# Part of a convolution moved to ScalarE and accumulating transfers, and a projection block moved between attention heads

## The chip, the cores and the metric

The kernel runs on one core of a Trainium2 chip. The metric is device time in microseconds of one execution. Three runs of the kernel before took 1779.26, 1779.52 and 1779.70 us; the median, 1779.52, is the time before. The engines are called as the profile calls them: PE (TensorE, matrix products; PEld its weight loads), DVE (VectorE), ACT (ScalarE), POOL (GpSimd) and SP (the queue that issues most transfers). Each engine works through its own list of instructions in order and waits on semaphores for the others.

## The reference

Two layers over 512 tokens of width 1024. Each layer normalises its input, projects it with one wide matrix, and feeds three token mixers whose outputs are gated and merged; then follow a feed-forward part and a gated embedding. What this case is about lies in the mixers:

```python
for i in range(DEPTH):
    h = rmsnorm(x, norm_mix[i])
    qa, ka, va, glu_in, qc, kc, vc, gates = split(h @ w_in[i])
    ya = diff_attention(qa, ka, va, ...)          # 4 heads, softmax difference, rmsnorm per head
    yb = conformer_conv(glu_in, ...)
    yc = neighbourhood_attention(qc, kc, vc, rpb[i])
    ga, gb, gc = split(sigmoid(gates))
    merged = ga * (ya @ w_br_a[i]) + gb * (yb @ w_br_b[i]) + gc * (yc @ w_br_c[i])
    x = x + merged @ w_o[i]
    ...

def conformer_conv(u, conv_w, conv_b, cln_g, cln_b):
    a, g = split(u)
    z = a * sigmoid(g)                            # 512 channels
    z = conv(z, conv_w) + conv_b                  # 31 taps, each channel by itself
    return silu(layernorm(z, cln_g, cln_b))
```

## The kernel before, in words

Activations lie transposed: 128 channels on the partitions, 512 tokens along the free axis, so a projection makes one 128x512 block at a time. A product in fp32 is made of three products of shorter numbers: every operand is split into a high half (ACT copies it with rounding, line 147) and a low half (DVE subtracts, line 161), and PE multiplies high by high, high by low, low by high (lines 181 to 183). `weights` fetches a block of weights by SP into a raw tile `wr` and splits it into `wh` and `wl`; there are three tiles of each tag, so the next block's split can start when PE or DVE has finished with the tile three blocks earlier.

A layer runs in this order: the gated input of the convolution (`glu`), neighbourhood attention (`natten`), the differential attention's projections and heads (`diff`), the gate blocks of the third mixer (`gate_c`, 8 blocks), two gate blocks of the second (`gate_b`), the product of the third mixer (`branch_c`, 8 blocks), two more blocks of `gate_b`, the product of the first mixer with its gates (`merge_a`, 8 blocks), the end of the convolution (`conv`) among the last four blocks of `gate_b`, then the merge, `w_o`, the feed-forward part and the embedding.

The order of PE's instructions is written by hand: it is the order of the Python code. Attention heads are cut into units, generators that a queue starts after so many blocks of products (`later`, `tick`), so pieces of a head stand between projection blocks. The order of DVE, ACT, POOL and SP is set by a scheduler that goes by the position in the program and by declared priorities; weights carry a priority of 400 positions ahead.

The 124 taps of the convolution (4 groups of 128 channels, 31 taps each) are DVE instructions: the first of a group at line 549, the others at line 164, one fused multiply and add of 128x512 into the group's sum. `taps` is a generator, and `background(after, n)` takes the next n taps from it and places them behind a given instruction. The table `BG` says how many each phase places. When `conv` starts, it takes the taps that are left, adds the four groups (`conv_ss`), splits the sum into `conv_rp`, and PE multiplies it with a matrix of ones (lines 579 and 580) for the mean.

A norm (`norm`) is four transposes on PE (line 217), a sum on DVE (line 220), a small step on DVE, a power on POOL (line 227, tile `rc`) and four transposes that spread the result (line 231). Transposes go through PSUM tiles of the tag `tr`, of which there are two; DVE frees such a tile when it has written the low half of what is in it (`diff_pt`).

Small tiles have a fixed number of buffers by tag: seven of the tag `t` (among them `diff_t`, the unnormalised output of a head, and `mergea_t`), two of the tag `b`. In the feed-forward part POOL issues transfers that add weights from memory to a tile (line 995).

Of the kernel before, what the change touches and what calls it, by code (L numbers as in the profile page):

```python
# [14 lines left out]
AF = mybir.ActivationFunctionType  # L15
ALU = mybir.AluOpType
# [4 lines left out]
P = 128  # L21
# [3 lines left out]
GR = 8  # L25
D = 1024
KD = 8
# [3 lines left out]
CON3W = 31  # L31
# [14 lines left out]
PAR_L = 8 + 8 + 8 + 1 + 4 + 4 + 4 + 4 * CON3W  # L46
PAR = L * PAR_L + 8
WARM = 8
BG = dict(glu=2, natten=1, values=3, diff=1, gatec=2, branchc=2, gateb=4, mergea=4, mergea2=2)
FIRST = (["v"] * 4 + ["pt"] * 2 + ["y", "b"], ["y"] * 5 + ["pt"] * 2 + ["b"])  # L50
EARLY = 6
QUARTERS = (2, 4, 6)
# [13 lines left out]
class Net:  # L66
# [229 lines left out]
    def build(self):  # L296
        nc, tc, a = self.nc, self.tc, self.a
        self.bufs = dict(wr=3, wh=3, wl=3, h=8, qk=2, kh=2, v=4, pt=2, y=5, z=5, x=4, t=7, rp=4,
                         e=4, a=3, r=2, rb=1, ss=1, sm=8, rc=4, b=2, s=8)
        self.bg, self.w_ahead = BG, 400  # L300
        self.pbufs = dict(mm=3, sc=2, tr=2, av=1)
# [130 lines left out]
    def layer(self, i, h, xsrc, xs):  # L432
        self.i, self.h = i, h
        zs, cs = [], []
        self.todo = self.taps(zs, cs)
        self.glu(zs)
        if i == 0:
            self.lambdas()
        yc, ya, yb = [], [], []
        sn, sd = {}, {}  # L440
        self.natten_in(0, sn, yc)
        self.drain(self.renorm)
        self.h = self.hs
        self.natten_v(sn)
        last = self.glu_last(zs)
        self.natten_in(1, sn, yc)
        next(last)
        self.natten_in(2, sn, yc)
        next(last)
        self.natten_in(3, sn, yc)  # L450
        acc, gb = [], []
        self.diff_in(0, sd, ya)
        self.diff_v(0, sd)
        self.diff_in(1, sd, ya)
        self.gate_c(acc, 0)
        self.diff_v(1, sd)
        self.diff_in(2, sd, ya)
        self.diff_in(3, sd, ya)
        for m in range(1, KD):
            self.gate_c(acc, m)  # L460
        for m in range(2):
            self.gate_b(gb, m, AF.Copy, None)
        for g in acc + gb:
            self.act(g, g, AF.Sigmoid, table="sigmoid")
        self.branch_c(acc, yc)
        for m in range(2, 4):
            self.gate_b(gb, m, AF.Sigmoid, "sigmoid")
        self.merge_a(ya, acc)
        conv = self.run(self.conv(cs, yb))
        pairs = self.inputs()  # L470
        for m in range(4, KD):
            self.gate_b(gb, m, AF.Sigmoid, "sigmoid")
            for n in ((0, 1), (2,), (3,), ())[m - 4]:
                self.input_block(pairs, n)
        self.drain(conv)
        mg = self.merge_b(yb, acc, gb)
        ws = self.pair_weights(4)
        x, h = self.w_o(mg, xsrc)
        self.input_pair(ws, pairs, 4)
        h = self.ffn(h, x)  # L480
        return self.ple(h, x, xs, self.inputs())
# [57 lines left out]
    def taps(self, zs, cs):  # L539

        for j, z in enumerate(zs):
            zf = z.rearrange("p a b -> p (a b)")
            c = self.sb("z", [P, 512])
            cs.append(c)
            for d in range(CON3W):
                w = self.par(self.i, "cw", j * CON3W + d)
                src = zf[:, d * GR:d * GR + 512]
                if d == 0:
                    yield self.nc.vector.tensor_scalar(c, src, w, self.par(self.i, "cb", j),
                                                       ALU.mult, ALU.add)  # L550
                else:
                    yield self.stt(c, src, w, c, ALU.mult, ALU.add)

    def background(self, after, n):

        ph, self.phase = self.phase, "conv"
        for _ in range(n):
            i = next(self.todo, None)
            if i is not None:
                self.tc.add_manual_dep(  # L560
                    i.ins, after.ins.name,
                    mybir.DependencyInfo(mybir.DependencyClass.NoSync, mybir.DependencyReason.DATA),
                    reason="background")
        self.phase = ph
# [203 lines left out]
    def gate_c(self, acc, m):  # L768
        self.phase = "gatec"
        ps = self.proj(OFF_G + 2 * D + m * P)  # L770
        if m % 2 == 0:
            acc += self.parts_of("x", [512], 2)
        self.background(self.act(acc[m], ps, AF.Copy), self.bg["gatec"])

    def branch_c(self, acc, ys):
        self.phase = "branchc"
        for m in range(KD):
            ps = self.ps("mm")
            self.gemm(ps, self.a["w_br_c"][self.i, m], ys)
            self.background(self.tt(acc[m], acc[m], ps, ALU.mult), self.bg["branchc"])  # L780

    def merge_a(self, ys, acc):
        self.phase = "mergea"
        for m in range(KD):
            ps = self.proj(OFF_G + m * P)
            g = self.sb("t", [P, 512])
            self.background(self.act(g, ps, AF.Sigmoid, table="sigmoid"), self.bg["mergea"])
            pb = self.ps("mm")
            self.gemm(pb, self.a["w_br_a"][self.i, m], ys)
            self.tt(g, g, pb, ALU.mult)  # L790
            self.background(self.tt(acc[m], acc[m], g, ALU.add), self.bg["mergea2"])

    def gate_b(self, gs, m, func, table):
        self.phase = "gateb"
        ps = self.proj(OFF_G + D + m * P)
        if m == 0:
            gs += [self.sb("kh", [P, 512]) for _ in range(2)]
        elif m % 2 == 0:
            gs += self.parts_of("v", [512], 2)
        self.background(self.act(gs[m], ps, func, table=table), self.bg["gateb"])  # L800

    def merge_b(self, ys, acc, gs):
        self.phase = "mergeb"
        out = []
        for m in range(KD):
            pb = self.ps("mm")
            self.gemm(pb, self.a["w_br_b"][self.i, m], ys)
            self.tt(gs[m], gs[m], pb, ALU.mult)
            self.tt(acc[m], acc[m], gs[m], ALU.add)
            mg = self.sb("y" if m < 5 else "v", [P, 2, 512], F32R)  # L810
            self.split(mg[:, 0, :], mg[:, 1, :], acc[m])
            out.append(mg)
        return out
# [656 lines left out]
```

## Time and profile before

| | |
|---|---|
| median of three runs | 1779.52 us |
| the profiled execution | 1779.11 us |
| its span, first to last instruction | 1777.3 us |
| mean granted TensorE clock | 0.998 |
| PE, PEld, DVE, ACT, POOL busy | 99%, 87%, 80%, 50%, 5% |
| DVE's taps of line 164 | 240, 747 ns each, 179.3 us |

The profile's rows read: start in us, duration in us, engine, line, operation, output and inputs by the program's names, shape; in brackets the idle time before the instruction and what ended it. The row of a wait says who waited for whom, then microseconds in total, the number of times and the longest. Tile names carry the phase in front: `conv_ss` is the tile `ss` made in the phase `conv`. Matmuls overlap, so that a row's duration of 0.39 us goes with a spacing of 0.227 us.

### The profile page before, as it was taken

The page shows a single profiled execution, that of the slowest core. Times are in us where ns is not written, and L with a number is a line of the kernel's source. Part 1 is how long each engine was busy: PE and PEld are TensorE (multiplying, and loading weights), DVE is VectorE, ACT ScalarE, POOL GpSimd, SP SyncE. Part 2 cuts the span into 40 slices and gives each one's busy share as a digit, 9 for nine tenths or more (in the row PEclk, how much of TensorE's full clock was granted, in tenths as well). Part 3 has the DMA queues.
Part 4 walks back from the last instruction along what each step waited for, and adds up shares of the span by engine and source line. Part 5 has one row for each costly group of instructions (what it writes and reads, how often), then busy time and mean ns, then how long its engine had stood idle before and what let it go on. Part 6 is the DMA issues. An engine that isn't in the chain of part 4 may idle for free.

```text
span 1777.3 us, 26765 instructions
## 1 busy us (share of the span) xinstructions
PE 1760.8 (99%) x9954; PEld 1544.1 (87%) x9954; DVE 1413.5 (80%) x2354; ACT 893.4 (50%) x1529; POOL 97.4 (5%) x114
## 2 busy tenths in 40 slices
PE   9999999999999999999999999999999999999998
PEld 7888878888899899998888887888888998989987
DVE  7967887998898587787776688779887985877776
ACT  5576555325565254454545765452356643534444
POOL 0000000000111010100000000000001110101000
PEclk9999999999999999999999999999999999999999
DMA  6577541334757366544446765423256673655332
GB/s 224 162 186 186 170 132 43 110 99 139 227 156 190 113 166 158 137 124 128 154 134 174 183 177 156 115 67 99 94 172 202 176 178 111 178 135 159 99 104 95
DMA packets 113698, 258.12 MB, mean 145 GB/s; under 512 B 14496, under 2 KB 23456, under 8 KB 113568
## 3 DMA queue, kind: packets, MB, share of 16 engines
q1 hardware_dynamic: 100176, 232.03, 42.7%
q0 software_dynamic: 12672, 23.07, 8.2%
q8 instruction: 78, 1.28, 0.3%
q10 hardware_dynamic: 720, 1.31, 0.2%
q14 instruction: 52, 0.43, 0.1%
HBM read 218.60 MB, written 7.34 MB: 127 GB/s over the span
## 4 chain that ended last, share of the span: by engine, by line
PE 90%; DVE 5%; ACT 1%; DMA 1%; issue 1%; SPq 0%; POOL 0%; ACTq 0%; DVEq 0%; POOLq 0%
PE ffn_mm L1025 4%; PE ffn_mm L1027 4%; PE ffn_mm L181 4%; PE ffn_mm L183 4%; PE ffn_mm L182 4%; PE ffn_mm L1026 4%; PE ffn_sc L1027 3%; PE ffn_sc L1025 3%; PE ffn_sc L1026 3%; PE mergea_mm L181 2%; PE mergea_mm L183 2%; PE mergea_mm L182 2%; PE gateb_mm L181 2%; PE wo_mm L181 2%; PE wo_mm L183 2%; PE wo_mm L182 2%
## 5 line engine op out<-in xcount | busy, mean ns | idle before, releaser
L164 DVE SCALAR_TENSOR_TENSOR conv_z<-glu_z,pre_par,conv_z 128x512 f32<-128x512 f32 x240 | 179.3, 747 | 3.0
L147 ACT ACTIVATE ffn_wh<-ffn_wr 128x1024 fp32r<-128x1024 f32 (+1 forms) x92 | 92.7, 1014 | 111.3 <-PE ffn_mm L182 80.7
L161 DVE TENSOR_TENSOR ffn_wl<-ffn_wr,ffn_wh 128x1024 fp32r<-128x1024 f32 (+1 forms) x92 | 107.3, 1172 | 5.4 <-ACT ffn_wh L147 4.9
L995 POOL DMA_DIRECT2D ffn_qk<-w_fu x88 | 77.9, 980 | 603.3 <-DMA ffn_qk<-w_fu 299.6
L161 DVE TENSOR_TENSOR ffn_t<-ffn_mm,wo_rb 128x512 f32<-128x512 f32 (+1 forms) x64 | 38.6, 604 | 67.8 <-PE ffn_mm L183 67.8
L147 ACT ACTIVATE mergea_wh<-mergea_wr 128x1024 fp32r<-128x1024 f32 (+1 forms) x32 | 27.1, 848 | 91.2 <-PE mergea_mm L182 71.7
L147 ACT ACTIVATE ffn_wh<-ffn_qk 128x1024 fp32r<-128x1024 f32 x44 | 46.7, 1061 | 36.7 <-PE ffn_mm L182 16.0
L161 DVE TENSOR_TENSOR ffn_wl<-ffn_qk,ffn_wh 128x1024 fp32r<-128x1024 f32 x44 | 53.8, 1223 | 10.8 <-ACT ffn_wh L147 10.8
L161 DVE TENSOR_TENSOR ffn_t<-ffn_t,ffn_t 128x512 f32<-128x512 f32 (+1 forms) x46 | 31.3, 680 | 32.0 <-ACT ffn_t L147 31.5
L161 DVE TENSOR_TENSOR diff_wl<-diff_wr,diff_wh 128x1024 fp32r<-128x1024 f32 x32 | 39.1, 1221 | 18.0 <-ACT diff_wh L147 12.4
L181 PE MATMUL ffn_mm<-ffn_v,ffn_wh 128*128 128x512 f32 x132 | 51.4, 389 | 0.0
L182 PE MATMUL ffn_mm<-ffn_v,ffn_wh 128*128 128x512 f32 x132 | 51.4, 389 | 0.0
L183 PE MATMUL ffn_mm<-ffn_v,ffn_wl 128*128 128x512 f32 x132 | 51.3, 389 | 0.0
L181 PE MATMUL ffn_mm<-ffn_y,ffn_wh 128*128 128x512 f32 x132 | 51.3, 389 | 0.0
L182 PE MATMUL ffn_mm<-ffn_y,ffn_wh 128*128 128x512 f32 x132 | 51.3, 389 | 0.0
L183 PE MATMUL ffn_mm<-ffn_y,ffn_wl 128*128 128x512 f32 x132 | 51.3, 389 | 0.0
L910 DVE TENSOR_REDUCE diff_s<-diff_sc 128x1 f32<-128x512 f32 x64 | 42.4, 683 | 10.0 <-PE diff_sc L819 10.0
L147 ACT ACTIVATE natten_e<-natten_e,natten_s 128x192 f32<-128x192 f32 (+1 forms) x88 | 39.3, 473 | 21.8 <-DVE natten_s L715 18.9
L1027 PE MATMUL ffn_mm<-wo_h,ffn_wl 128*128 128x256 f32 x176 | 49.8, 283 | 0.0
L1027 PE MATMUL ffn_sc<-wo_h,ffn_wl 128*128 128x256 f32 x176 | 49.8, 283 | 0.0
L1026 PE MATMUL ffn_mm<-wo_h,ffn_wh 128*128 128x256 f32 x176 | 49.8, 283 | 0.0
L1026 PE MATMUL ffn_sc<-wo_h,ffn_wh 128*128 128x256 f32 x176 | 49.8, 283 | 0.0
(882 smaller groups left out, 6477.3 us busy)
## 6 DMA issues: line engine op xcount, KB each, us to landing
ffn_qk<-w_fu POOLq DMA_DIRECT2D x88, 256.0 KB, 5.7
ffn_wr<-w_fg SPq DMA_DIRECT2D x44, 512.0 KB, 3.8
ffn_wr<-w_fd SPq DMA_DIRECT2D x32, 448.0 KB, 3.8
ffn_r<-w_fu SPq DMA_DIRECT2D x44, 256.0 KB, 4.3
ffn_qk<-w_fg SPq DMA_DIRECT2D x44, 256.0 KB, 4.0
ffn_qk<-w_fu SPq DMA_DIRECT2D x44, 256.0 KB, 4.4
natten_wr<-w_in SPq DMA_DIRECT2D x16, 512.0 KB, 4.1
diff_wr<-w_in SPq DMA_DIRECT2D x16, 512.0 KB, 3.8
```

Source lines behind the costliest of these rows:

```text
L147: i = self.nc.scalar.activation(out, in_, func, **kw)
L161: return self.nc.vector.tensor_tensor(out, a, b, op)
L164: return self.nc.vector.scalar_tensor_tensor(out, a, s, b, op0, op1)
L181: mm(out, wh, ah, start=first, stop=False)
L182: mm(out, wh, al, start=False, stop=False)
L183: mm(out, wl, ah, start=False, stop=last)
L910: nc.vector.tensor_reduce(out=m[:, u:u + 1], in_=sc, op=ALU.max, axis=AX.X, negate=True)
L995: nc.gpsimd.dma_start(q, wu[:, lo], accum_op=ALU.add)
L1025: mm(out, wh[:, c], bh, start=first and k == 0, stop=False, skip_group_check=True)
L1026: mm(out, wh[:, c], bl, start=False, stop=False, skip_group_check=True)
L1027: mm(out, wl[:, c], bh, start=False, stop=k == 3, skip_group_check=True)
```

## The change

Three things are changed.

The block `gate_c(1)`, which stood behind all four heads' projections, now stands between the projections of head 2 and head 3. The number of PE's instructions is the same; the attention units keep their distance in blocks.

Of the channel groups 2 and 3 the first twelve taps each (`LINKS = 24`) leave DVE. For the first of them ACT writes the scaled block with the bias into a tile of the tag `b` (the list `far`). For the others ACT writes the scaled block into a tile of the tag `t`, and POOL issues a transfer of 256 KB that adds it to `far`. The two groups alternate, and each transfer waits for the one before it in its own group. `link` emits one such step at the end of each block of `gate_c`, `gate_b` and `branch_c` and in `merge_a`; what is left is emitted when the taps reach group 2. DVE's taps of these groups then start at tap 12 on `far`. DVE keeps 100 taps of 124.

The table of taps per phase is lower in `diff` (0 instead of 1), `gatec` (1 instead of 2), `branchc` (1 instead of 2) and `gateb` (2 instead of 4).

```diff
-BG = dict(glu=2, natten=1, values=3, diff=1, gatec=2, branchc=2, gateb=4, mergea=4, mergea2=2)
+BG = dict(glu=2, natten=1, values=3, diff=0, gatec=1, branchc=1, gateb=2, mergea=4, mergea2=2)
+LINKS = 24
...
-        self.todo = self.taps(zs, cs)
+        self.todo, self.links = self.taps(zs, cs), self.chain(zs)
...
         self.diff_in(2, sd, ya)
+        self.gate_c(acc, 1)
         self.diff_in(3, sd, ya)
-        for m in range(1, KD):
+        for m in range(2, KD):
             self.gate_c(acc, m)
...
-            c = self.sb("z", [P, 512])
+            if j < 2:
+                c, n = self.sb("z", [P, 512]), 0
+            else:
+                for _ in self.links:
+                    pass
+                c, n = self.far[j - 2], LINKS // 2
             cs.append(c)
-            for d in range(CON3W):
+            for d in range(n, CON3W):
...
+    def chain(self, zs):
+
+        self.far = [self.sb("b", [P, 512]) for _ in range(2)]
+        for n in range(LINKS):
+            d, j = divmod(n, 2)
+            w = self.par(self.i, "cw", (j + 2) * CON3W + d)
+            src = zs[j + 2].rearrange("p a b -> p (a b)")[:, d * GR:d * GR + 512]
+            if d == 0:
+                self.act(self.far[j], src, AF.Identity, scale=w, bias=self.par(self.i, "cb", j + 2))
+            else:
+                t = self.sb("t", [P, 512])
+                self.act(t, src, AF.Copy, scale=w)
+                self.nc.gpsimd.dma_start(self.far[j], t, accum_op=ALU.add)
+            yield
+
+    def link(self):
+
+        ph, self.phase = self.phase, "conv"
+        next(self.links, None)
+        self.phase = ph
...
         self.background(self.act(acc[m], ps, AF.Copy), self.bg["gatec"])
+        self.link()
...
             self.background(self.tt(acc[m], acc[m], ps, ALU.mult), self.bg["branchc"])
+            self.link()
...
             self.background(self.act(g, ps, AF.Sigmoid, table="sigmoid"), self.bg["mergea"])
+            self.link()
...
         self.background(self.act(gs[m], ps, func, table=table), self.bg["gateb"])
+        self.link()
```

How the lists of the engines differ is shown at three places of layer 1. In these rows the number behind a tile's name tells buffers of one name apart; lines of the changed program are higher by 1 at the top and by some 30 further down.

The first place is DVE's list round head 0's norm. `diff_pt` is the low half of the transposed probabilities, `diff_rp` are steps of the rotation of queries and keys, `conv_z` a tap. Before:

```order
L161 TENSOR_TENSOR gatec_wl_2487<-gatec_wr_2485,gatec_wh_2486 128x1024
L161 TENSOR_TENSOR diff_rp_2139<-diff_rp_2139,diff_kh_2151 128x512
L161 TENSOR_TENSOR diff_rp_2230<-diff_rp_2230,diff_r_1315 128x512
L164 SCALAR_TENSOR_TENSOR conv_z_2147<-glu_z_324,pre_par_67,conv_z_2147 128x512
L161 TENSOR_TENSOR diff_rp_2231<-diff_rp_2231,diff_r_1317 128x512
L164 SCALAR_TENSOR_TENSOR diff_a_2283<-diff_e_2289,diff_s_2278,diff_a_2283 128x512
L161 TENSOR_TENSOR diff_rp_2230<-diff_rp_2230,diff_rp_2231 128x512
L161 TENSOR_TENSOR diff_pt_2311<-diff_tr_2306,diff_pt_2311 128x512
L161 TENSOR_TENSOR diff_pt_2319<-diff_tr_2314,diff_pt_2319 128x512
```

And now:

```order
L162 TENSOR_TENSOR diff_rp_2136<-diff_rp_2136,diff_kh_2146 128x512
L162 TENSOR_TENSOR gatec_wl_2482<-gatec_wr_2480,gatec_wh_2481 128x1024
L947 RECIPROCAL diff_s_2258<-diff_s_2258 128x1
L162 TENSOR_TENSOR diff_pt_2291<-diff_tr_2286,diff_pt_2291 128x512
L165 SCALAR_TENSOR_TENSOR diff_s_2258<-diff_s_2258,glu_nlam_445,diff_sm_1800 128x1
L162 TENSOR_TENSOR diff_pt_2299<-diff_tr_2294,diff_pt_2299 128x512
L165 SCALAR_TENSOR_TENSOR diff_a_2263<-diff_e_2269,diff_s_2258,diff_a_2263 128x512
```

Head 3's rotation, the tap and the softmax row `diff_a` no longer stand between the weight split and `diff_pt`.

The second place is the end of head 2 and of head 3, on ACT and on POOL. On ACT, between the copy of head 2's output (`diff_t`) and the split of the next weights (`branchc_wh`), before:

```order
L147 ACTIVATE diff_ss_2831<-diff_av_2686 128x512
L147 ACTIVATE diff_t_2830<-diff_av_2686,glu_subg_447 128x512
L147 ACTIVATE diff_a_2872,diff_sm_2344<-diff_sc_2868,diff_s_2867 128x512
L147 ACTIVATE diff_e_2878,diff_s_2867<-diff_sc_2874,diff_s_2867 128x512
L147 ACTIVATE branchc_wh_3026<-branchc_wr_3025 128x512
L147 ACTIVATE gateb_kh_2911<-gateb_mm_2837 128x512
```

And now, where `conv_t` are the copies of the links:

```order
L148 ACTIVATE diff_t_2833<-diff_av_2685,glu_subg_447 128x512
L148 ACTIVATE conv_t_2840<-glu_z_836,pre_par_67 128x512
L148 ACTIVATE conv_t_2922<-glu_z_327,pre_par_67 128x512
L148 ACTIVATE conv_t_2997<-glu_z_836,pre_par_67 128x512
L148 ACTIVATE conv_t_3031<-glu_z_327,pre_par_67 128x512
L148 ACTIVATE conv_t_3071<-glu_z_836,pre_par_67 128x512
L148 ACTIVATE conv_t_3095<-glu_z_327,pre_par_67 128x512
L148 ACTIVATE diff_a_2878,diff_sm_2409<-diff_sc_2874,diff_s_2873 128x512
L148 ACTIVATE diff_e_2884,diff_s_2873<-diff_sc_2880,diff_s_2873 128x512
L148 ACTIVATE branchc_wh_3036<-branchc_wr_3035 128x512
L148 ACTIVATE gateb_kh_2917<-gateb_mm_2843 128x512
```

Six copies have come between `diff_t` and head 3's exponential `diff_a`. POOL's list before holds nothing but the powers of the norms here (heads 0 to 3 and the convolution):

```order
L227 TENSOR_TENSOR diff_rc_2276<-diff_sm_2274,pre_power_104 128x4
L227 TENSOR_TENSOR diff_rc_2580<-diff_sm_2578,pre_power_104 128x4
L227 TENSOR_TENSOR diff_rc_2865<-diff_sm_2863,pre_power_104 128x4
L227 TENSOR_TENSOR diff_rc_3153<-diff_sm_3151,pre_power_104 128x4
L227 TENSOR_TENSOR conv_rc_3926<-conv_sm_3924,pre_power_104 128x4
```

And now, from head 2's power to head 3's:

```order
L228 TENSOR_TENSOR diff_rc_2871<-diff_sm_2869,pre_power_104 128x4
L573 DMA conv_b_1863<-conv_t_3031 128x512
L573 DMA conv_b_1864<-conv_t_3071 128x512
L573 DMA conv_b_1863<-conv_t_3095 128x512
L573 DMA conv_b_1864<-conv_t_3137 128x512
L573 DMA conv_b_1863<-conv_t_3172 128x512
L573 DMA conv_b_1864<-conv_t_3196 128x512
L573 DMA conv_b_1863<-conv_t_3229 128x512
L228 TENSOR_TENSOR diff_rc_3168<-diff_sm_3166,pre_power_104 128x4
```

Seven links have come between the two powers.

The third place is DVE's list from the weights of `gate_b(4)`, the first block behind `merge_a`, to the sum of the convolution. `pin` is the input embedding, whose small blocks stand there too. Before:

```order
L161 TENSOR_TENSOR gateb_wl_3806<-gateb_wr_3804,gateb_wh_3805 128x1024
L164 SCALAR_TENSOR_TENSOR conv_z_3460<-glu_z_836,pre_par_67,conv_z_3460 128x512
L161 TENSOR_TENSOR gatec_x_2765<-gatec_x_2765,mergea_t_3698 128x512
L164 SCALAR_TENSOR_TENSOR conv_z_3460<-glu_z_836,pre_par_67,conv_z_3460 128x512 x3
L161 TENSOR_TENSOR pin_wl_3857<-pin_wr_3855,pin_wh_3856 128x256
L164 SCALAR_TENSOR_TENSOR conv_z_3460<-glu_z_836,pre_par_67,conv_z_3460 128x512
L161 TENSOR_TENSOR conv_ss_3783<-conv_ss_3783,conv_z_3460 128x512
```

And now, from the second split of `pin` on; seven taps stand ahead of it behind the split for `gate_b(4)`:

```order
L162 TENSOR_TENSOR pin_wl_3917<-pin_wr_3915,pin_wh_3916 128x256
L162 TENSOR_TENSOR mergea_t_3794<-mergea_t_3794,mergea_mm_3800 128x512
L162 TENSOR_TENSOR pin_e_3838<-pin_t_3835,pin_e_3837 128x512
L162 TENSOR_TENSOR gatec_x_2766<-gatec_x_2766,mergea_t_3794 128x512
L165 SCALAR_TENSOR_TENSOR conv_b_1864<-glu_z_836,pre_par_67,conv_b_1864 128x512
L162 TENSOR_TENSOR pin_e_3844<-pin_t_3841,pin_e_3843 128x512
L165 SCALAR_TENSOR_TENSOR conv_b_1864<-glu_z_836,pre_par_67,conv_b_1864 128x512 x4
L162 TENSOR_TENSOR gateb_wl_3933<-gateb_wr_3931,gateb_wh_3932 128x1024
L165 SCALAR_TENSOR_TENSOR conv_b_1864<-glu_z_836,pre_par_67,conv_b_1864 128x512
L162 TENSOR_TENSOR conv_ss_3827<-conv_ss_3827,conv_b_1864 128x512
L162 TENSOR_TENSOR conv_rp_3832<-conv_ss_3827,conv_rp_3831 128x512
```

More taps stand ahead of the sum, and the weight split of the next block, `gate_b(5)`, has come ahead of the last tap.

## The prediction

> **What bounds the kernel now.** I read the page's span and engine shares first, then the waits of PE, then the chain through the largest of them, then timelines round the places that the change rewrites.
>
> ```profile
> span 1777.3 us, 26765 instructions
> PE 1760.8 (99%) x9954; PEld 1544.1 (87%) x9954; DVE 1413.5 (80%) x2354; ACT 893.4 (50%) x1529; POOL 97.4 (5%) x114
> ...
> PE 90%; DVE 5%; ACT 1%; DMA 1%; issue 1%; SPq 0%; POOL 0%; ACTq 0%; DVEq 0%; POOLq 0%
> ```
>
> PE is busy in all but some 17 us of 1777.3, and the change leaves PE its work. So no work taken from DVE is worth its own duration: only PE's waits count, those that go and those that come. These are the ones that are there (microseconds in total, times, longest):
>
> ```profile
> PE diff_tr L231 <- DVE diff_pt L161: 6.0, 2, 3.0
> PE diff_mm L614 <- DVE natten_y L161: 1.1, 2, 0.7
> ...
> PE diff_tr L867 <- DVE diff_a L164: 0.9, 2, 0.5
> ```
>
> Each occurs once a layer ("2"). All times below are of layer 1; layer 2 repeats it 879 us later. The chain shows why L231, the transposes of head 0's norm, is late:
>
> ```profile
> 226.99 0.68 DVE diff_rp L161
> 227.67 0.66 DVE conv_z L164
> 228.34 0.60 DVE diff_rp L161
> 228.94 0.66 DVE diff_a L164
> 229.60 0.60 DVE diff_rp L161
> 230.20 0.61 DVE diff_pt L161
> 230.81 0.14 issue
> 230.95 0.62 PE diff_tr L231 x4
> ```
>
> Both buffers with the tag "tr" are held until DVE has read them (diff_pt), and before diff_pt stand three rope rows (diff_rp) of head 3's query, a tap (conv_z) and a softmax row.
>
> **What goes away.** In the new order gate_c(1) runs ahead of head 3's projections, so these rope rows come after diff_pt, and gate_c and diff emit fewer taps. The rows from 226.99 up to 230.20 are 3.2 us; without them diff_pt begins near 227 and L231's buffer is free when PE gets there at 230.95 − 3.0 = 227.9. I take the whole 3.0 a layer: **−6.0**. L867 loses its 0.5 (the softmax row is then not behind taps): **−0.9**. L614 waits for a natten_y behind taps of the attention phase, which lose one per projection; half of the 1.1: **−0.5**.
>
> The stall at L231 cost more in layer 2. In these rows the columns after the stretch are its length, then PE, PEld, DVE, ACT, POOL busy with counts, then the granted TensorE clock:
>
> ```profile
> 231.30:234.70 3.40, 3.40 (x18) 2.81 (x17) 3.09 (x6) 2.05 (x5) 0.00 (x0) 1.00 0.88 252
> 1110.00:1113.40 3.40, 3.40 (x12) 2.79 (x11) 3.00 (x6) 1.54 (x4) 0.00 (x0) 0.54 0.80 237
> ```
>
> After the same 3.0 us idle the clock stayed at 1.00 once and fell to 0.54 once: (1 − 0.54) × 3.40 = 1.6 us. That goes too: **−1.6**. Gains together −9.0.
>
> The moved block's own work is 24 matmuls, one weight transfer, one ACT and one DVE split; it keeps its size and comes earlier. Head 3's q and k come one block (24 × 0.227 = 5.4 us) later, with their rotations and stacks on SP behind the block's weight transfer. The last stack and its first reader:
>
> ```profile
> 252.80 1.24 SPq L653 DMA_DIRECT2D diff_x<-diff_rp  x2
> ...
> 270.35 0.39 PE L819 MATMUL diff_sc<-diff_qk 128*128 128x512 f32 x1
> ```
>
> They leave 16.3 us, less 5.4, against a few us of transfer: cost nothing. The cover would go if SP were 8 us late.
>
> **What is moved to ACT and POOL.** Each layer gets 24 ACT copies of 128x512 (0.5 to 0.7 us; ACT is at 50%) and 22 accumulating transfers of 256 KB on POOL's software queue, and DVE loses 24 taps. The old trace has accumulating transfers of 256 KB on that queue, though from HBM (L995, in the FFN); SBUF to SBUF it has plain ones on SP:
>
> ```profile
> L995 POOL DMA_DIRECT2D ffn_qk<-w_fu x88: 862/883/1243, 453.9 to 1643.7; - x88
> ...
> DMA to landing us min/median/max: 3.9/5.7/8.6
> ```
> ```profile
> natten_x<-natten_x SPq DMA_DIRECT2D x4, 256.0 KB, 2.9
> ```
>
> So 2.9 to 8.6 us from issue to landing. I take 4 to 4.5 for a lone link, because queue, size and operation agree with L995, whose 5.7 was met amid heavy weight traffic and in pairs, and up to 6 for the second of two issued together. The links of a chain wait for each other's landing. Two places make others wait.
>
> First, ACT after head 2 (second column: duration):
>
> ```profile
> 282.85 0.60 ACT L147 ACTIVATE diff_ss<-diff_av 128x512 f32<-128x512 f32 x1 [1.03 <-PE diff_av L183]
> 283.35 0.68 ACT L147 ACTIVATE diff_t<-diff_av,glu_subg 128x512 f32<-128x512 f32 x1
> 287.44 0.69 ACT L147 ACTIVATE diff_a<-diff_sc,diff_s 128x512 f32<-128x512 f32 x1 [3.41 <-DVE diff_s L910]
> ...
> 290.08 0.58 ACT L147 ACTIVATE gateb_kh<-gateb_mm 128x512 f32<-128x512 f32 x1
> ```
>
> Now six link copies stand between diff_t and the exponential diff_a. The sixth reuses the slot of the first, so it waits for that link to land: issued about 284.7 (283.35, diff_t, one copy), landed about 288.9, and the exponential starts near 289.3 instead of 287.44. gateb_kh, which frees the PSUM buffer that gate_b(1) needs, then ends near 291.9 instead of 290.66; PE, which needs it there, loses 1.2: **+2.4** for two layers. Bounds: nothing, if the link takes 2.9 (the slot is free at 287.6); 5.7 a layer at 8.6. A gain is excluded, since nothing ahead of the exponential became shorter.
>
> Second, POOL before head 3's norm:
>
> ```profile
> 313.05 0.68 ACT L147 ACTIVATE diff_t<-diff_av,glu_subg 128x512 f32<-128x512 f32 x1
> ```
> ```profile
> 318.88 1.01 POOL L227 TENSOR_TENSOR diff_rc<-diff_sm,pre_power 128x4 f32<-128x4 f32 x1 [30.25 <-DVE diff_sm L164]
> ```
> ```profile
> 321.03 0.60 PE L231 MATMUL diff_tr<-pre_ident,diff_rc 128*128 128x128 f32 x4
> ```
>
> The power diff_rc was alone on POOL. Now four links stand ahead of it, whose copies follow diff_t: the first two issue near 314.4 and 315.3 (diff_t's end, a copy, then 0.88 of issue), the third waits for the first, the fourth for the second, which lands at 319.7 to 321.9; I take 321. Then come 0.9 of issue and 1.01 of power, and L231 can start near 323.1 instead of 321.03: 2.1 a layer, **+4.2**. Behind these links ACT also holds gate_b's weight copies; the stall covers them. Bounds: nothing at 2.9 (the power done by 320.2), about 5 at 8.6.
>
> **The convolution's sum** is the largest term. After merge_a PE's list has gate_b(4), and right behind it two matmuls L579 and L580 over the summed taps:
>
> ```profile
> 393.45 1.22 DVE L161 TENSOR_TENSOR gateb_wl<-gateb_wr,gateb_wh 128x1024 fp32r<-128x1024 f32 x1
> ...
> 399.21 0.69 DVE L161 TENSOR_TENSOR conv_ss<-conv_ss,conv_z 128x512 f32<-128x512 f32 x1
> ...
> 402.20 0.68 DVE L161 TENSOR_TENSOR conv_rp<-conv_ss,conv_rp 128x512 fp32r<-128x512 f32 x1
> ```
> ```profile
> 400.68 0.62 ACT L147 ACTIVATE conv_rp<-conv_ss 128x512 fp32r<-128x512 f32 x1
> ...
> 405.85 1.06 ACT L147 ACTIVATE gateb_wh<-gateb_wr 128x1024 fp32r<-128x1024 f32 x1 [3.50 <-issue]
> ```
> ```profile
> 405.82 0.39 PE L579 MATMUL conv_tr<-conv_rp,pre_onesr 128*128 128x512 f32 x1
> 406.05 0.39 PE L580 MATMUL conv_tr<-conv_rp,pre_onesr 128*128 128x512 f32 x1
> ```
>
> Before, five taps stand between this gateb_wl and the sum, and conv_rp is ready at 402.9, 3.2 us ahead of the second matmul. Although the change does 24 fewer taps on DVE, it takes away more background places before merge_a (diff 8, gate_c 8, branch_c 8, gate_b 8): 96 places for 100 taps, where there were 128 for 124. So 13 taps now stand there, and DVE's order puts the next block's weight split ahead of the last of them. That split follows gateb_wh, which starts at 405.85 when gate_b(4) ends. So: gateb_wh to 406.9, gateb_wl 407.3 to 408.4, last tap 409.1, sum 409.9, ACT's high half 410.6, DVE's low half 411.3; the second matmul starts near 411.35 instead of 406.05. That is 5.3 a layer, **+10.6**. Bounds: 4.3, if every step follows at once without the gaps of the old rows; 7, if the raw weights land late. Nothing or less is excluded as long as that split is ahead of the tap.
>
> New stalls cool the clock as the old one did. Five idle us I expect to cost 1.6 almost every time (1.35 on average, two layers: **+2.7**), those of 2 us less than a third of the time (2 × 1.6 × 0.3: **+1.0**).
>
> The clock has a rule in the Trainium skill, "TensorE: Matmul & The Clock Gate", section "What's actually happening": half rate after at least one idle window of about 3.4 us, the windows running freely. The 0.54 after 3.0 us idle is against that as a strict bound. By it the 1.6 would be no gain, a stall of 4.9 us would cool in (4.9 − 3.4)/3.4 = 44% of cases, an estimate from that page, and the sum would be 0.7 lower (+1.6 − 1.3 − 1.0).
>
> Sum: −9.0 + 2.4 + 4.2 + 10.6 + 2.7 + 1.0 = +11.9. The profiled execution took 1779.11, 0.41 under the median of the runs; 1779.11 + 11.9 = **1791**.
>
> **Rivals.** (1) Links land within about 3 us. Both link terms and their 1.0 go: 1791 − 7.6 = 1783. SP's 2.9 speaks for it, the minimum of 3.9 in 88 transfers of L995 against it. The Trainium skill, "DMA: Bandwidth & Descriptors", section "Anatomy of one DMA — SWDGE (gpsimd) path", fits 2.0 us plus bytes/436e3, an estimate of 2.6 for 256 KB, which is this rival; the 5.7 measured here disagrees. (2) Not slower: the sum is in time after all, because DVE, 24 taps lighter, reaches it before the split is due. It decides at the sum's start: by 404.5 (405.82 − 0.62 − 0.69). Then 10.6 + 2.7 go: 1791 − 13.3 = 1778. The order of DVE's rows speaks against it. (3) The change does what it says: stalls gone, links hidden, sum in time: 1779.1 − 9.0 = 1770. It needs (1) and (2) at once. (4) Links take 6 to 8.6 us, the upper half of L995's range: the link terms grow from 3.3 a layer towards 10.7, which gives 1796 to 1806.
>
> **How the numbers follow.** The main case has 0.58 (its own range 1785 to 1796), (1) 0.18, (2) 0.07, (3) 0.05, (4) 0.12. What a measurement here can tell from no change is 0.2%, 3.6 us. Faster is (3) and a little of (2), 0.06; same the rest of (2) and the lowest of (1), 0.08; slower 0.86. The range from 1781 to 1800 leaves out (2), (3) and the upper half of (4).
>
> **What would show it.** In the new trace PE should have no wait at head 0's L231, L867 and L614; waits of about 5 us at the second matmul of the sum for DVE's conv_rp, of about 2 us at head 3's L231 for POOL, of about 1 us at gate_b(1) for ACT's gateb_kh; and the clock below 0.9 just behind the first. The conv_b links should show 4 to 6 us to landing. I am wrong if the sum starts before 404.5, or if landings are far from 4 to 6.

## The result, and the profile after

The changed kernel took 1789.93 us (median of four runs, 1789.46 to 1790.38) against 1779.61 us for the kernel before: a ratio of 1.0057, with a 95% interval of 1.004 to 1.0075. It is slower by 10.3 us; 1791 had been forecast. The profiled execution took 1789.94 us, its span is 1787.9 us, and the mean granted clock 0.997.

The page of the changed kernel shows what the shares hide: DVE does 30 us less, PE as much as before, and the span is 10.6 us longer.

```profile
span 1787.9 us, 26859 instructions
PE 1762.9 (99%) x9954; PEld 1544.3 (86%) x9954; DVE 1383.3 (77%) x2306; ACT 920.7 (51%) x1577; POOL 136.7 (8%) x158
```

The waits of PE are a new list (line numbers are 1 higher at the top of the program, 28 to 32 higher further down, so L232 is the old L231 and L607 the old L579):

```profile
PE conv_tr L607 <- ACT conv_rp L148: 9.2, 2, 4.6
PE diff_tr L232 <- POOL diff_rc L228: 3.4, 2, 1.7
PE diff_mm L642 <- DVE natten_y L162: 2.6, 2, 1.5
PE gateb_mm L182 <- ACT gateb_kh L148: 1.8, 2, 0.9
```

The waits for diff_pt (6.0) and diff_a (0.9) are gone. In their place stand the sum of the convolution, head 3's norm, the product of the values, and gate_b(1), each once a layer.

The sum first. DVE, ACT and PE round it in layer 1 of the changed kernel, each from the timeline of its engine:

```profile
402.33 3.11 DVE L165 SCALAR_TENSOR_TENSOR conv_b<-glu_z,pre_par,conv_b 128x512 f32<-128x512 f32 x4
405.36 1.22 DVE L162 TENSOR_TENSOR gateb_wl<-gateb_wr,gateb_wh 128x1024 fp32r<-128x1024 f32 x1
406.50 0.74 DVE L165 SCALAR_TENSOR_TENSOR conv_b<-glu_z,pre_par,conv_b 128x512 f32<-128x512 f32 x1
407.27 0.69 DVE L162 TENSOR_TENSOR conv_ss<-conv_ss,conv_b 128x512 f32<-128x512 f32 x1
408.66 0.69 DVE L162 TENSOR_TENSOR conv_rp<-conv_ss,conv_rp 128x512 fp32r<-128x512 f32 x1 [0.70 <-ACT conv_rp L148]
```
```profile
403.92 1.06 ACT L148 ACTIVATE gateb_wh<-gateb_wr 128x1024 fp32r<-128x1024 f32 x1 [3.98 <-PE gateb_mm L183]
...
408.00 0.63 ACT L148 ACTIVATE conv_rp<-conv_ss 128x512 fp32r<-128x512 f32 x1 [2.54 <-DVE conv_ss L162]
```
```profile
408.68 0.80 PE L607 MATMUL conv_tr<-conv_rp,pre_onesr 128*128 128x512 f32 x1 [4.58 <-ACT conv_rp L148]
409.41 0.80 PE L608 MATMUL conv_tr<-conv_rp,pre_onesr 128*128 128x512 f32 x1
```

This is the forecast chain step by step: the high half of the next weights starts when PE is done with gate_b(4) (the releaser is PE), then the low half, the last tap, the sum, the two halves of the sum. The chain is not alone, though. The high half is done at 404.98, and the low half starts at 405.36, right behind four taps that keep DVE busy until 405.44. With the split behind the last tap the sum would still have been late, by some 3.6 us (an estimate from these rows), so the place of the split is not the whole cause of the stall, and the leftover taps alone account for much of it. No run has the one without the other.

PE stands still for 4.58 us. The second matmul starts 0.06 us after the low half of the sum is written (408.66 + 0.69 = 409.35). Both matmuls take 0.80 instead of 0.39 us: the clock has dropped. Here are two windows behind the stall in layer 1 and two in layer 2, with PE's busy time second and the granted clock third from the end:

```profile
407.46:410.87 3.41, 2.19 (x5) 1.46 (x6) 1.82 (x4) 0.63 (x1) 0.00 (x0) 0.50 0.12 38
410.87:414.28 3.41, 3.41 (x10) 2.64 (x9) 3.39 (x7) 3.07 (x6) 0.00 (x0) 0.50 0.01 2
1294.92:1298.33 3.41, 3.40 (x7) 2.44 (x8) 2.52 (x5) 1.06 (x2) 0.00 (x0) 0.50 0.00 0
1298.33:1301.74 3.41, 3.41 (x16) 2.79 (x15) 3.28 (x7) 3.41 (x7) 0.00 (x0) 1.00 0.21 30
```

Layer 1 runs through two such windows at half clock, layer 2 through one.

The two waits on the links are there too. On ACT after head 2 the sixth copy waits 1.25 us for the landing of the first link, and the exponential starts behind it. On POOL after head 3 the third and the fourth link wait 2.14 and 1.40 us for landings, and the power, and with it PE, comes after them:

```profile
283.79 0.72 ACT L148 ACTIVATE conv_t<-glu_z,pre_par 128x512 f32<-128x512 f32 x1 [1.25 <-DMA conv_b<-conv_t]
284.42 0.67 ACT L148 ACTIVATE diff_a<-diff_sc,diff_s 128x512 f32<-128x512 f32 x1
```
```profile
310.93 1.78 POOL L573 DMA_DIRECT2D conv_b<-conv_t  x2 [19.59 <-ACT conv_t L148]
314.85 0.86 POOL L573 DMA_DIRECT2D conv_b<-conv_t  x1 [2.14 <-DMA conv_b<-conv_t]
317.11 0.86 POOL L573 DMA_DIRECT2D conv_b<-conv_t  x1 [1.40 <-DMA conv_b<-conv_t]
317.68 1.34 POOL L228 TENSOR_TENSOR diff_rc<-diff_sm,pre_power 128x4 f32<-128x4 f32 x1
```
```profile
319.08 0.65 PE L232 MATMUL diff_tr<-pre_ident,diff_rc 128*128 128x128 f32 x4 [1.70 <-POOL diff_rc L228]
```

The links took this long from issue to landing (view of line 573):

```profile
DMA to landing us min/median/max: 3.2/3.9/7.9
```

In the pair above the next links start 3.9 and 5.6 us after the issues (310.93 to 314.85, 311.54 to 317.11). The landings themselves are earlier: ACT's copies that reuse the tiles of these two links start at 314.29 and 316.55, and the trace has the landings at 314.20 and 316.47, 3.3 and 4.9 us after the issues. So POOL's next link starts 0.6 us after the landing that it waits for, ACT's copy 0.1 us.

### The profile page after: what moved, and what is told of

Its sections match the earlier page's. It is cut to its first block, busy times and chain, and to the rows that moved or that the text cites. A ratio compares the mean times of both kernels' runs of the same rounds, so it can differ in the third digit from the quotient of the medians.

```text
span 1787.9 us, 26859 instructions
## 1 busy us (share of the span) xinstructions
PE 1762.9 (99%) x9954; PEld 1544.3 (86%) x9954; DVE 1383.3 (77%) x2306; ACT 920.7 (51%) x1577; POOL 136.7 (8%) x158
## 3 DMA queue, kind: packets, MB, share of 16 engines
q10 hardware_dynamic: 720, 1.31, 0.2%
## 4 chain that ended last, share of the span: by engine, by line
PE 82%; issue 9%; DVE 3%; DMA 3%; ACT 2%; POOL 0%; SPq 0%; POOLq 0%; ACTq 0%; DVEq 0%
PE ffn_mm L1057 4%; PE ffn_mm L1059 4%; PE ffn_mm L183 4%; PE ffn_mm L184 4%; PE ffn_mm L182 4%; PE ffn_mm L1058 4%; PE ffn_sc L1059 3%; PE ffn_sc L1057 3%; PE ffn_sc L1058 3%; PE mergea_mm L183 2%; PE mergea_mm L182 2%; PE mergea_mm L184 2%; DMA conv_b<-conv_t 2%; PE wo_mm L184 2%; PE wo_mm L183 2%
## 5 line engine op out<-in xcount | busy, mean ns | idle before, releaser
L165 DVE SCALAR_TENSOR_TENSOR conv_z<-glu_z,pre_par,conv_z 128x512 f32<-128x512 f32 x120 | 89.7, 747 | 1.3
L573 POOL DMA_DIRECT2D conv_b<-conv_t x44 | 39.8, 953 | 620.5 <-ACT conv_t L148 529.8
L162 DVE TENSOR_TENSOR ffn_wl<-ffn_qk,ffn_wh 128x1024 fp32r<-128x1024 f32 x44 | 53.8, 1223 | 10.8 <-ACT ffn_wh L148 10.8
L165 DVE SCALAR_TENSOR_TENSOR conv_b<-glu_z,pre_par,conv_b 128x512 f32<-128x512 f32 x76 | 56.6, 749 | 4.2 <-DMA conv_b<-conv_t 2.9
```

Of the source, the lines that this page charges most:

```text
L162: return self.nc.vector.tensor_tensor(out, a, b, op)
L165: return self.nc.vector.scalar_tensor_tensor(out, a, s, b, op0, op1)
L573: self.nc.gpsimd.dma_start(self.far[j], t, accum_op=ALU.add)
```

## The experiments

The expectations speak of a "theory" and a "rival"; the theory is the account of the prediction, amended by the runs ahead of each.

**Background places put back.** The changed kernel with one number of the table changed.

```diff
-BG = dict(glu=2, natten=1, values=3, diff=0, gatec=1, branchc=1, gateb=2, mergea=4, mergea2=2)
+BG = dict(glu=2, natten=1, values=3, diff=0, gatec=1, branchc=1, gateb=4, mergea=4, mergea2=2)
```

> The changed kernel with gate_b's background places put back from 2 to 4, so that 104 places serve the 100 taps that DVE keeps; links and moved block stay. Theory of the places: the sum of the convolution is late only because taps are left over when merge_a ends; now none is, PE's wait of 4.74 + 0.50 us a layer at the sum and the low clock behind it (2.4 and 1.3 us) go, 1789.9 - 10.5 - 3.7 = about 1775.7, faster than the kernel before. The waits at gate_b(1) (1.05 us) and at head 3's norm (1.86 us) stay. Rival, the links delay the sum (their chain lands late, or ACT is held by their copies): it stays late by several us, 1785 or more.

Measured: 1776.56 us, ratio 0.9982 (0.9972 to 0.9991) to the kernel before (1780.17 on that chip). The waits of PE:

```profile
PE diff_tr L232 <- POOL diff_rc L228: 3.3, 2, 1.7
PE diff_mm L642 <- DVE natten_y L162: 3.2, 2, 1.8
PE gateb_mm L182 <- ACT gateb_kh L148: 1.8, 2, 0.9
```

The wait for conv_rp is gone and the two of the links are as they were. Eight more places make the difference between slower and a little faster; the links do not delay the sum.

**The lower table alone.** The kernel before with the changed kernel's table, without links and move.

```diff
-BG = dict(glu=2, natten=1, values=3, diff=1, gatec=2, branchc=2, gateb=4, mergea=4, mergea2=2)
+BG = dict(glu=2, natten=1, values=3, diff=0, gatec=1, branchc=1, gateb=2, mergea=4, mergea2=2)
```

> The kernel before with the lower table of places alone: 96 places for 124 taps, no links, block not moved. Theory of the places: 28 taps are left when merge_a's last background is done, and 26 of them stand in one row behind the split for gate_b(5); the wait at the sum is then 5.24 us plus 25 more taps of 0.667 us = 21.9 us a layer, and the clock behind it is low for some 2 us; the wait at head 0's norm shrinks from 3.18 to about 1 to 2 because one tap has left the rows ahead of diff_pt. 1779.6 + 2 x (21.9 + 2 - 1.5) = about 1824, between 1818 and 1830. Rival, the links delay the sum: without links it is in time, and the time stays within 5 us of the kernel before.

Measured: 1825.09 us, ratio 1.0256 (1.0241 to 1.0272).

```profile
PE conv_tr L579 <- ACT conv_rp L147: 47.9, 2, 24.0
...
PE diff_tr L231 <- DVE diff_pt L161: 1.1, 2, 0.6
```

Leftover taps are paid one by one at the sum: none there costs nothing, one behind the weight split 4.6 us of wait, 26 of them 24.0 us, 0.78 us a tap. That is the tap's own 0.75 us and a gap of 0.03; each of these taps needs the sum of the one before. The second row was less than the expectation's 1 to 2 us a layer: without the move, the wait at head 0's norm fell from 3.0 to 0.6 us.

**The move alone.**

```diff
         self.diff_in(2, sd, ya)
+        self.gate_c(acc, 1)
         self.diff_in(3, sd, ya)
-        for m in range(1, KD):
+        for m in range(2, KD):
```

> The kernel before with gate_c(1) moved ahead of head 3 and nothing else. Theory of the rows: the wait at head 0's norm came from head 3's rope rows in front of diff_pt, so the move alone takes away 3.18 us a layer and the 1.5 us of low clock in layer 2: 1779.6 - 7.8 = about 1771.8. The waits of L614 and L867 (0.6 to 0.9 us a layer each) may stay. Rival, DVE's load as such: as DVE still does 124 taps, its backlog shows at this norm again or at another place, and the time stays within 3 us of the kernel before.

Measured: 1773.51 us, ratio 0.9965 (0.9953 to 0.9978). The move takes the wait at head 0's norm from 3.0 to 0.6 us a layer by itself, and no new wait of that size comes up:

```profile
PE diff_mm L615 <- DVE natten_y L161: 1.2, 2, 0.8
PE diff_tr L231 <- DVE diff_pt L161: 1.1, 2, 0.6
```

**No taps in diff, without and with the move.** The same edit of the table, which leaves 128 places for 124 taps, in the kernel before and in the kernel with the move.

```diff
-BG = dict(glu=2, natten=1, values=3, diff=1, gatec=2, branchc=2, gateb=4, mergea=4, mergea2=2)
+BG = dict(glu=2, natten=1, values=3, diff=0, gatec=2, branchc=2, gateb=4, mergea=5, mergea2=2)
```

Without the move:

> The kernel before with no tap placed in diff and five in merge_a; nothing moved, no links. From the run with the lower table alone the wait at head 0's norm is 0.7 instead of 3.18 without the move. Theory: 1780.2 - 2 x 2.45 - 1.45 (low clock) - 1.26 (L867) + 1.5 (product of the values) = about 1774; move and taps take away the same wait, so together they give little more than either. Rival, the two add up: this alone is worth under 3 us, 1777 or more.

With it:

> The kernel before with gate_c(1) moved, no tap placed in diff and five instead of four in merge_a (128 places for 124 taps); no links. Theory: against the move alone (1773.5) the rest of the wait at head 0's norm (2 x 0.7), L867 (2 x 0.6) and a wait for diff_v (2 x 0.4) go, and natten_y at the product of the values comes later, as it does in the changed kernel (1.32 and 1.65 instead of 1.0 and 0.5): 1773.5 - 3.4 + 1.5 = about 1771.6. Rival, without links DVE's fifth tap a block in merge_a is too much: new waits in merge_a, over 1776.

Measured: 1771.07 us without the move (ratio 0.9956, 0.9939 to 0.9972) and 1769.82 us with it (0.9948, 0.9933 to 0.9963), against 1779.5. With the move the largest wait of PE is this:

```profile
PE diff_mm L615 <- DVE natten_y L161: 2.0, 2, 1.0
```

Neither list has a wait for diff_pt or diff_a. So the two edits take away one and the same wait, and they do not add up. The second, two numbers of a table, is enough. Five taps instead of four behind the gate of each block of merge_a bring no wait there. The wait for diff_a goes in every run without taps in diff and stays with the move alone (0.9), as the prediction had it.

**The changed kernel without its move.** Only the move is undone.

```diff
         self.diff_in(2, sd, ya)
-        self.gate_c(acc, 1)
         self.diff_in(3, sd, ya)
-        for m in range(2, KD):
+        for m in range(1, KD):
```

> The changed kernel with gate_c(1) back behind the four heads; the links and the lower table stay. Theory from the runs so far: a table without taps in diff takes the wait at head 0's norm away by itself (to 0.7 us in the run with the table alone, to nothing with five taps in merge_a), so the move is worth at most 0.7 a layer here: 1790 to 1792. Rival, the account in the prediction: the move takes the rope rows from ahead of diff_pt, and without it the 3.0 us a layer and the low clock of one of the two come back, about 1797.

Measured: 1792.31 us, ratio 1.0069 (1.0054 to 1.0085), against 1789.93 for the changed kernel with it.

```profile
PE conv_tr L606 <- ACT conv_rp L148: 9.2, 2, 4.6
...
PE diff_tr L232 <- DVE diff_pt L162: 1.1, 2, 0.6
```

The kernel before took 1780.41 us on this chip and 1779.61 on the other, so against it the two are 11.9 and 10.3 us slower, and their intervals overlap. In the changed kernel the move is worth 1 us of waiting at this norm in the trace and at most some 2 us of time, not the 7.6 us that go with it in the prediction's account.

**The links alone.** The kernel before with the changed kernel's `chain`, `link` and their calls, its own table, and no move.

```diff
-        self.todo = self.taps(zs, cs)
+        self.todo, self.links = self.taps(zs, cs), self.chain(zs)
...
+            self.link()
```

> The kernel before with the 24 links alone, the block not moved and the table of places as before (128 places for 100 taps). Theory: DVE's rows round head 0's norm are as before, so its wait of 3.0 us stays; the sum is early; the links cost their two waits, 1.05 - 0.32 us at gate_b(1) and 1.86 us at head 3's norm a layer: 1779.6 + 5.2 = about 1785. Rival, less work on DVE is worth something by itself: 24 fewer taps shorten the wait at head 0's norm, and the time is at or below 1779.6.

Measured: 1805.89 us, ratio 1.0149 (1.0133 to 1.0164), 21 us over the expectation and slower than the links with everything else. The waits of PE, and DVE where merge_a begins:

```profile
PE diff_tr L232 <- POOL diff_rc L228: 9.0, 4, 2.9
PE diff_tr L232 <- DVE diff_pt L162: 6.0, 2, 3.0
PE mergea_mm L184 <- DVE mergea_wl L162: 4.6, 2, 3.4
PE mergea_mm L182 <- DVE mergea_t L162: 2.9, 1, 2.9
```
```profile
344.72 2.33 DVE L165 SCALAR_TENSOR_TENSOR conv_b<-glu_z,pre_par,conv_b 128x512 f32<-128x512 f32 x3 [7.08 <-DMA conv_b<-conv_t]
346.96 0.68 DVE L162 TENSOR_TENSOR mergea_wl<-mergea_wr,mergea_wh 128x512 fp32r<-128x512 f32 x1
347.56 5.47 DVE L165 SCALAR_TENSOR_TENSOR conv_b<-glu_z,pre_par,conv_b 128x512 f32<-128x512 f32 x7
```

The expectation had forgotten when `taps` comes to group 2. With the higher table tap 62 is reached in branch_c, not in merge_a, and there the generator emits all links that are left at once. Eleven of them then stand in two chains, each link waiting for the landing of the one before, and DVE waits 7.08 us for the end of a chain, with merge_a's weight splits queued behind its taps. The norms cost more than expected as well: the power waits behind links at head 1 and at head 3, four times in all, 9.0 us where 3.7 had been expected. By the spacing of PE's matmuls the waits in merge_a (7.9 us), the norms (5.9 more) and the low clock behind both (7.7 more than in the kernel before) make up the 21 us. So the links ask for a lower table than the old one, which keeps group 2 back until its chain has landed; the changed kernel's table is lower than they ask, since with eight places more (the first experiment) the chains are still in time for PE. One thing is as expected: DVE's rows at head 0's norm are the old ones, and so is the wait of 3.0 us.

**Twelve links.** The changed kernel with half the links, emitted only in gate_c and gate_b, and a table with 116 places for the 112 taps.

```diff
-BG = dict(glu=2, natten=1, values=3, diff=0, gatec=1, branchc=1, gateb=2, mergea=4, mergea2=2)
-LINKS = 24
+BG = dict(glu=2, natten=1, values=4, diff=0, gatec=1, branchc=1, gateb=4, mergea=5, mergea2=2)
+LINKS = 12
...
             self.background(self.tt(acc[m], acc[m], ps, ALU.mult), self.bg["branchc"])
-            self.link()
...
             self.background(self.act(g, ps, AF.Sigmoid, table="sigmoid"), self.bg["mergea"])
-            self.link()
```

> The changed kernel with 12 links instead of 24, emitted in gate_c and gate_b alone, and a table with places enough (values 4, gate_b 4, merge_a 5: 116 places for 112 taps). After head 2 three copies stand ahead of the exponential and none waits for a landing; after head 3 two links stand ahead of the power and none waits for a landing. Theory, it is the wait for landings that costs, not the links: both link waits (0.74 and 1.84 us a layer) go, 1776.6 - 5.2 = about 1771.5. Rival, the links as such load POOL or the transfers: one or both waits stay and the time is over 1775.

Measured: 1771.88 us, ratio 0.9958 (0.9943 to 0.9973).

```profile
PE natten_sc L739 <- DVE natten_x L162: 1.7, 1, 1.7
...
PE gateb_mm L182 <- ACT gateb_kh L148: 0.3, 2, 0.2
```

Both link waits of PE are gone (gate_b(1) is back at its old 0.3), while twelve links still run on POOL. This run has fewer copies and transfers too, so by itself it does not tell them from the waiting. The rows of the changed kernel do: the wait for a landing there is 1.25 us on ACT where PE loses 0.9, and 2.14 + 1.40 us on POOL where PE loses 1.7. Without the waiting neither PE wait would be left, and it was the waiting for landings in front of other work that cost. The first row, in layer 1 alone, comes where a fourth tap a step now stands in natten_v (three taps are in the chain into it). Against 1769.82 without any link the links bring nothing here; the two tables differ as well.

**Two tries at the product of the values.** The changed kernel had made this wait longer (0.7 to 1.5 at most). Both tries stand on the kernel with the move and no taps in diff (1769.82). The first declares natten_y earlier, the second swaps two PSUM tiles.

```diff
-        self.split(y[rs, 0], y[rs, 1], av[rs])
-        self.tt(y[rs, 1], y[rs, 1].bitcast(F32), av[ro], ALU.add)
+        with ahead():
+            self.split(y[rs, 0], y[rs, 1], av[rs])
+            self.tt(y[rs, 1], y[rs, 1].bitcast(F32), av[ro], ALU.add)
```

> As the moved block with no taps in diff, and natten_unit's last two steps, which write natten_y and free PE's PSUM buffer, are declared 200 positions ahead. Theory: the wait at the product of the values (L614 before; 1.3 and 1.6 us) is one of the order of DVE's rows, in which a rope row, ACT's diff_kh and a softmax row come before natten_y, and goes: about 3 us less than without the declaration, 1768.6. Rival: rows that natten_y passes become late instead (diff_v, the weights of the next block) and the time stays within 1 us.

```diff
-        av = self.ps(("av", "mm")[u])
+        av = self.ps(("av", "mm")[1 - u if pr == 3 else u])
```

> As the moved block with no taps in diff and five in merge_a (1769.8), and in the last pair of natten's heads the two units swap their PSUM tiles: the first takes the tag mm, the second av. Theory: the product of the values waits only because the second unit's natten_y holds one of the three mm tiles; the first unit's natten_y is done 7 us earlier, so the wait of 1.14 and 1.16 us goes, 1769.8 - 2.3 = about 1767.5, and nothing takes its place, since the first user of av after it comes with head 0's product. Rival: the wait comes from another of the mm tiles or from the weights behind it, and stays; or it moves to the product that needs av. Then 1769 to 1771.

Measured: 1770.67 us (ratio 0.9952, 0.9937 to 0.9967) and 1770.24 us (0.9944, 0.9932 to 0.9957): no gain over 1769.82 in either. The wait with the declaration, and the first row with the swap:

```profile
PE diff_mm L615 <- DVE natten_y L161: 2.0, 2, 1.1
```
```profile
PE natten_mm L753 <- ACT diff_rp L147: 2.1, 2, 1.1
```

The declaration did not move the rows at that place, so it told nothing about their order. The swap took this wait away and put one of the same size 13 us earlier, where the first unit now needs a tile with the tag mm that a projection still holds (ACT's diff_rp reads it). This suggests that the wait belongs to the three mm tiles and moves with whoever comes fourth; no run had a fourth tile, so that is not shown.

## Why the prediction was right, and where it was not

The table sets the prediction's terms beside the traces. The measured column is the spacing of PE's matmuls over their usual spacing at that place, changed kernel minus kernel before, both layers together.

| term | predicted us | measured us |
|---|---|---|
| wait at head 0's norm | −6.0 | −6.4 |
| low clock behind it, layer 2 | −1.6 | −1.6 |
| L867, the transposes of diff_a | −0.9 | −1.3 |
| L614, the product of the values | −0.5 | +1.5 |
| gate_b(1), behind the link copies | +2.4 | +1.5 |
| head 3's norm, behind the links | +4.2 | +3.7 |
| the convolution's sum | +10.6 | +10.5 |
| low clock behind the sum | +2.7 | +3.7 |
| low clock behind head 3's norm | +1.0 | 0 |
| the first matmuls of the program | 0 | −1.1 |
| together | +11.9 | +10.5 |

The two profiled executions differ by 10.8 us. That the total is so close is luck in part: L614 came out 2.0 us higher than predicted, and the two waits on links (1.4 lower) and the first matmuls (1.1) offset it. The row on the first matmuls is no part of the change: their excess differs by up to 1.3 us among the profiled executions of all these kernels. The main case came true in its waits, their places and their releasers. The links were faster than it had them: the lone ones at the two places that count landed 3.2 to 3.3 us after their issue (median of all 3.9) where 4 to 4.5 had been taken. That is close to rival (1), yet its gain did not come: 3.2 us was late there too. Rival (2) needed the sum to start 1.31 us before PE gets there; PE was ready at 408.68 − 4.74 = 403.94, and the sum started at 407.27.

At head 3's norm the second link landed 4.9 us after its issue where 5.7 had been taken, but the first was issued 0.3 us later than assumed, and POOL started the next link only 0.6 us after the landing, for which the prediction had nothing. The errors nearly cancel, which is luck: the norm was 0.25 us a layer cheaper. At gate_b(1) the exponential started 1.43 us before PE was ready (286.90 − 1.05 − 284.42) where it had started 2.95 before (290.71 − 0.32 − 287.44), so it was late by 1.5 us rather than 1.9, and a copy of the next weights that used to wait 0.65 us took up some of that.

The step that failed in sign is L614. The prediction gave it half of the old wait because a tap would leave the rows ahead of natten_y. The tap did leave, and the scheduler then put other rows there. The chain of the changed kernel into that matmul:

```profile
176.38 0.64 ACT diff_kh L148
...
177.05 0.69 DVE diff_rp L162
...
177.77 0.69 DVE natten_y L162
...
178.50 0.70 DVE diff_s L942
...
179.22 0.69 DVE natten_y L162
...
180.05 0.47 PE diff_mm L642
```

ACT now does the high half of a key (diff_kh) ahead of natten_y, and a softmax row (diff_s) stands between natten_y's two steps, where a rope row stood. PE reached the matmul earlier, and natten_y was not earlier by as much. This place had not been read in the new order. Taking the taps out of diff is enough for it, without links or move: in total the wait is 1.1 us before, 1.2 with the move alone and 1.9 where only the taps of diff go to merge_a.

The term that was right in size but not in cause is head 0's norm: the prediction gave the whole 3.0 us to the moved block, and named the missing tap only beside it. The runs show that either edit alone takes most of it (2.4 us each, or all of it with no tap in diff and five in merge_a), and that in this kernel the move is worth at most some 2 us.

The low clock was mis-sized at two places: 3.7 instead of 2.7 behind the sum (2.4 in layer 1, 1.3 in layer 2), nothing instead of 1.0 behind stalls of 1.9 us. The prediction took every drop as 1.6 us and gave it a chance by the length of the stall. The runs show that a drop lasts one window or two, that stalls below 2 us bring none, and that for stalls near 3 us it hangs on where the stall lies, as stands below. So it was a matter of luck that layer 2 had a drop at head 0's norm to lose. The Trainium skill's rule ("TensorE: Matmul & The Clock Gate", section "What's actually happening") gave 44% for a stall of 4.9 us at the sum, by the prediction's estimate; the stall was 4.58 us, and the clock dropped in both layers.

## What to carry to other kernels

Where one engine is busy 99% of the time, work taken from another engine is worth only the waits it ends, and it is worth reading the list of those waits before moving anything: here two numbers in a table of places (diff 1 to 0, merge_a 4 to 5) give 1771 us, and with the moved block 1770 us, while the links bring nothing beside it. If background work is placed by counts, compare the number of places with the number of pieces ahead of every point where the pieces must be done, since what is left over is paid in full there. A chain of transfers that wait for each other must not stand on an in-order queue in front of something that another engine needs: what it costs is the landing time, not the transfer.

## What the runs showed of the hardware

**The clock is set every 3.413 us by what PE did in the 3.413 us before.** In every trace the recorded changes of the clock lie whole steps of 3.413 us apart. With the links alone the clock drops at 230.69, 353.57, 1124.98, 1220.55 and 1258.10, 36, 226, 28 and 11 steps apart; it is always 1.00 or 0.50. Cut along these steps, the traces sort themselves by PE's busy time. These are two windows and the ones behind them, in the kernel before and in the run with the links alone (PE's busy time second, granted clock third from the end):

```profile
229.05:232.46 3.41, 1.51 (x9) 1.37 (x10) 3.41 (x6) 0.63 (x1) 0.00 (x0) 1.00 0.89 206
232.46:235.88 3.42, 3.42 (x20) 2.93 (x19) 3.04 (x7) 2.88 (x6) 0.00 (x0) 1.00 0.86 264
```
```profile
1217.14:1220.55 3.41, 1.37 (x7) 0.79 (x5) 0.28 (x1) 1.91 (x3) 1.42 (x2) 1.00 0.75 201
1220.55:1223.97 3.42, 2.87 (x9) 2.48 (x10) 2.24 (x3) 2.04 (x3) 2.29 (x3) 0.50 0.83 142
```

In the twelve traces all 12 windows at full clock in which PE was busy for at most 1.37 us are followed by a window at half clock, and none of the others, which have 1.51 us or more. So what counts is how a stall lies to the steps. Layer 1 of the kernel before had 1.12 us of its 3.0 us stall in one window and 1.90 in the next, and the clock stayed; in layer 2 the same stall lay almost whole in one window, and it dropped. No wait of PE up to 2 us was followed by a drop, six of the eight between 2.6 and 3.4 us were, and all six of 4.6 us and more.

A drop that PE ran through for one window cost 1.3 to 1.7 us, one of two windows 1.9 to 3.0. Behind 24 us of stall it was no more (2.6 and 1.6) than behind 4.6 (2.4 and 1.3). The Trainium skill's rule ("TensorE: Matmul & The Clock Gate", section "What's actually happening") asks for an idle window of 3.4 us. That is more than was needed here: 2.04 us of idle time in one window were enough, and 1.90 were not.

**An accumulating transfer of 256 KB within SBUF** lands 3.9 us after its issue in the median (3.2 to 7.9), on the queue on which an accumulating transfer of the same size from HBM takes 5.8 in the same trace; the Trainium skill's fit ("DMA: Bandwidth & Descriptors", section "Anatomy of one DMA — SWDGE (gpsimd) path") gives 2.6, an estimate below the smallest of the 44.
